# State-space layer of a two-layer trunk: weight split and C product taken off GpSimd, decay matrices from one masked addition per head

## The chip, the core and the metric

The kernel runs on one core of one Trainium2 chip. The core has a matrix engine (TensorE, PE in the profile; its weight loads, PEld, overlap its matmuls), a vector engine (VectorE, DVE), a scalar engine for activations (ScalarE, ACT), a general engine (GpSimd, POOL) and a queue that issues most transfers (SyncE, SP). Each engine works through its own instructions in order and waits on semaphores for the others. The metric is the time of one execution on the device in microseconds (us).

## The reference, cut to what matters

The reference is a trunk of two layers over 256 latent tokens and 256 context tokens of width 1024. Layer 0 is attention and a gated feed-forward net; layer 1 is a bidirectional state-space mixer (32 heads, 4 groups, state 128, chunks of 128 tokens) and a feed-forward net. The change is in the mixer. For each direction and chunk it computes

```python
cum = jnp.cumsum(dtc * a, axis=1)
seg = cum[:, :, None] - cum[:, None, :]
decay = jnp.exp(jnp.where(lower, seg, -jnp.inf))
cb = jnp.einsum('bign,bjgn->bijg', cc, bc)
w = cb[..., None] * decay * dtc[:, None]
y = jnp.einsum('bijgr,bjgrp->bigrp', w, xc)
y = y + jnp.einsum('bign,bgrpn->bigrp', cc, s) * jnp.exp(cum)[..., None]
to_end = jnp.exp(cum[:, -1:] - cum) * dtc
s = s * jnp.exp(cum[:, -1])[..., None, None] + jnp.einsum('bjgr,bjgn,bjgrp->bgrpn', to_end, bc, xc)
```

`dt` is a softplus of a projection, `x`, `B` and `C` come from a centred convolution and a silu. The context is scanned first and leaves the state `s`; the latent tokens go on from it. After that `y + d*x` is multiplied by `silu(z)`, normed, and projected.

## The kernel before, in words

Every weight matrix arrives as a stream of units of 128x1024 numbers (`load_raw`, line 244, on SyncE's queue, five buffers). Matmuls keep fp32 accuracy with a split in two parts: ScalarE copies a unit rounded (L232), and a second engine subtracts (L234), so that each step of a GEMM is three matmuls (L289 to L291). `pool_split` lists the units whose subtraction is on GpSimd instead of VectorE: all of the attention input, every second unit of the state-space input (`si`), the first two of the last feed-forward input (`f1i`). Two split buffers `ws` exist in the state-space layer.

The `si` GEMM has 41 column blocks: one for `dt`, four for B, four for C, then sixteen pairs of an x block (512 tokens) and a z block (256). A unit is one block. When a block is done, its function runs: `ssm_dt`, `ssm_B`, `ssm_C`, `ssm_x`, `ssm_z`. TensorE's side work (transposes, states, outputs) is put in a timed queue with `later` and comes between the steps of the GEMM.

`ssm_dt` makes `dt` with a polynomial, the cumulative sums `cum` with scans (L1117), stores them in memory (L1119), and makes the columns `ust` that are used as scalars per row. `ssm_x` for pair j asks for the spread cumulative sums of the next two heads (`cum_load`, L1183, tile `cumb`, four buffers), makes the convolved `xs` (L1019 twice with the tile `cacc`, then L1082), and calls `head_mats` for its two heads. Later it transposes `xs` on TensorE (`xps`, L1231), copies it (`xl`, `xw`, L1237), makes the state (`sps`, L1247), and adds up the output `y` from sixteen matmuls (L1264): eight with `wm` (the decay matrices times `CB`), eight with `ctl` (C times a decay). `finish_pair` then makes `u` from `y`, `xs` and `z`, its square for the norm (added on GpSimd, L1280) and the split `vv` for the output product `so`.

`head_mats` for one head makes four sums `xx` of cumulative sum, row column and mask (L1195, VectorE, 128x128 each), one exponential over them (L1198, ScalarE), two exponentials into `wm` (L1200, L1201), three into `ctl` (L1204 to L1206), the product of `ctl` with C on GpSimd (L1207), and on VectorE the sum of the two masked parts (L1208) and the product with `CB` (L1210). `wm` and `ctl` have four buffers, two pairs; a pair's matrices can be written when `y` of two pairs before has been read.

The order of the instructions on each engine is set by the tile framework from the program's order and priorities (the weight stream has a higher one), not by a table.

## Time and profile before

| | us |
|---|---|
| median of 3 runs (1229.09 to 1230.51) | 1229.57 |
| span of the profiled execution | 1228.7 |
| state-space input product, all blocks (first to last `si` matmul) | 681.8 to 968.1 |
| first and last `xs` (pairs 0 and 15) | 750.8 and 971.4 |
| output product `so` | 970.2 to 1021.6 |

The profile is one execution. A busy time is the union of an engine's instructions. The chain of work that ended last is followed back from the last instruction: each of its rows gives a start, a length, the engine and the line. A group's row gives the busy time and the mean of one instruction in ns, and behind the bar the time that its engine stood idle before it and who ended that. A tile's or line's row gives the shortest, median and longest duration in ns. A stretch's row gives its bounds, its length, and each engine's busy time in it with the number of instructions.

### The profile page before, as it was taken

To read this page: it belongs to the slowest core of one execution; us is meant where nothing else is said; L and a number is where in the kernel's file an instruction comes from. 1 tells how busy PE (TensorE), PEld (TensorE's weight loads), DVE (VectorE), ACT (ScalarE), POOL (GpSimd) and SP (SyncE) were. 2 spreads that over 40 slices of the span, in tenths; PEclk is the share of its full clock that TensorE was granted. 3 is DMA by queue.
4 is the path that set the end of the run, shared out by engine and by line. 5 is a ranking of instruction groups with operands and counts; after the bars stand their busy time and mean duration, and the time that the engine had idled before them with its cause. 6 is when DMAs were issued, how large, how long until landed. Compare 5 with 4: busy or idle time off the path is not lost.

```text
span 1228.7 us, 17902 instructions
## 1 busy us (share of the span) xinstructions
PE 1167.3 (95%) x6899; PEld 950.4 (77%) x6903; DVE 858.9 (70%) x1411; ACT 596.3 (49%) x1072; POOL 177.3 (14%) x122
## 2 busy tenths in 40 slices
PE   8999999999999999999999988888888899999997
PEld 5765556678888888888888976666666698999997
DVE  4568856545776877655663699888888766777654
ACT  4366655543633333332222756566656546555542
POOL 3331221100000000000000232333334202000000
PEclk9999999999999999999999998999999999999999
DMA  8622142422344555536663335433333255776651
GB/s 313 240 97 93 58 148 70 137 69 86 119 152 158 168 158 163 163 112 214 216 209 123 91 105 134 106 104 103 103 103 103 84 175 173 228 235 212 183 182 58
DMA packets 56677, 176.64 MB, mean 144 GB/s; under 512 B 5840, under 2 KB 15632, under 8 KB 56592
## 3 DMA queue, kind: packets, MB, share of 16 engines
q1 hardware_dynamic: 56016, 174.98, 45.1%
q8 instruction: 54, 0.88, 0.3%
q10 hardware_dynamic: 576, 0.52, 0.1%
q14 instruction: 31, 0.25, 0.1%
HBM read 174.37 MB, written 1.11 MB: 143 GB/s over the span
## 4 chain that ended last, share of the span: by engine, by line
PE 73%; DVE 20%; ACT 2%; DMA 2%; issue 1%; POOL 0%; DVEq 0%; ACTq 0%; POOLq 0%
PE f0i L289 6%; PE f0i L291 6%; PE f0i L290 6%; DVE xx L1195 4%; PE f1i L289 3%; PE f1i L290 3%; PE f1i L291 3%; PE ai L289 3%; PE ai L291 2%; PE y L1264 2%; PE f0o L291 2%; PE f0o L289 2%; PE ai L290 2%; PE f0o L290 2%; DVE ws L234 2%; DVE cacc L1019 2%
## 5 line engine op out<-in xcount | busy, mean ns | idle before, releaser
L232 ACT ACTIVATE ws<-raw 128x1024 fp32r<-128x1024 f32 x215 | 227.1, 1056 | 260.9 <-PE f0i L291 87.6
L234 DVE TENSOR_TENSOR ws<-raw,ws 128x1024 fp32r<-128x1024 f32 x175 | 214.4, 1225 | 101.4 <-ACT ws L232 100.5
L234 POOL TENSOR_TENSOR ws<-raw,ws 128x1024 fp32r<-128x1024 f32 x40 | 99.2, 2482 | 322.9 <-ACT ws L232 307.2
L289 PE MATMUL f0i<-h,ws 128*128 128x512 f32 x336 | 131.4, 391 | 0.0
L290 PE MATMUL f0i<-h,ws 128*128 128x512 f32 x336 | 130.9, 389 | 0.0
L291 PE MATMUL f0i<-h,ws 128*128 128x512 f32 x336 | 130.8, 389 | 0.0
L289 PE MATMUL si<-h,ws 128*128 128x256 f32 (+1 forms) x312 | 111.8, 358 | 5.6 <-DVE cacc L1019 5.1
L409 DVE SCALAR_TENSOR_TENSOR macc<-raw,cpad,macc 128x1024 f32<-128x1024 f32 x70 | 89.1, 1281 | 31.0 <-DMA raw<-mod_w 30.8
L291 PE MATMUL si<-h,ws 128*128 128x256 f32 (+1 forms) x312 | 106.5, 341 | 3.3 <-DVE ws L234 2.0
L290 PE MATMUL si<-h,ws 128*128 128x256 f32 (+1 forms) x312 | 106.3, 341 | 0.0
L289 PE MATMUL f1i<-h,ws 128*128 128x256 f32 x352 | 100.1, 286 | 0.0
L290 PE MATMUL f1i<-h,ws 128*128 128x256 f32 x352 | 99.6, 283 | 0.0
L291 PE MATMUL f1i<-h,ws 128*128 128x256 f32 x352 | 99.5, 283 | 0.0
L566 POOL TENSOR_TENSOR h<-ht,h 128x256 fp32r<-128x256 f32 x12 | 9.8, 820 | 460.3 <-DVE ws L234 363.5
L289 PEld LDWEIGHTS si<-h,ws 128*128 128x128 f32 x312 | 60.0, 192 | 18.3 <-issue 12.0
L289 PEld LDWEIGHTS f0i<-h,ws 128*128 128x128 f32 x336 | 63.1, 188 | 14.1 <-ACT hid L573 0.8
L291 PEld LDWEIGHTS f0i<-h,ws 128*128 128x128 f32 x336 | 63.1, 188 | 13.2
L290 PEld LDWEIGHTS f0i<-h,ws 128*128 128x128 f32 x336 | 63.1, 188 | 13.0
L289 PEld LDWEIGHTS f1i<-h,ws 128*128 128x128 f32 x352 | 67.9, 193 | 0.8 <-ACT hid L573 0.4
L291 PEld LDWEIGHTS si<-h,ws 128*128 128x128 f32 x312 | 59.6, 191 | 11.1 <-DVE ws L234 2.4
L1195 DVE SCALAR_TENSOR_TENSOR xx<-cumb,ust,msk 128x128 f32<-128x128 f32 x128 | 67.9, 579 | 0.0
L290 PEld LDWEIGHTS f1i<-h,ws 128*128 128x128 f32 x352 | 67.8, 192 | 0.0
(303 smaller groups left out, 2824.4 us busy)
## 6 DMA issues: line engine op xcount, KB each, us to landing
raw<-mod_w SPq DMA_DIRECT2D x80, 512.0 KB, 3.7
raw<-w_f0i SPq DMA_DIRECT2D x44, 512.0 KB, 3.9
raw<-w_f1i SPq DMA_DIRECT2D x44, 512.0 KB, 3.9
raw<-w_si SPq DMA_DIRECT2D x41, 512.0 KB, 3.6
raw<-w_f0o SPq DMA_DIRECT2D x22, 512.0 KB, 4.7
raw<-w_f1o SPq DMA_DIRECT2D x22, 512.0 KB, 3.7
raw<-w_ai SPq DMA_DIRECT2D x18, 512.0 KB, 4.2
raw<-mod_s SPq DMA_DIRECT2D x16, 512.0 KB, 5.3
```

The source lines that it names most:

```text
L232: ops = [nc.scalar.activation(out=hi, in_=r, func=AF.Copy)]
L234: ops.append(eng.tensor_tensor(out=s[:, 1].rearrange("p a b -> p (a b)"), in0=r, in1=hi.bitcast(F32), op=ALU.subtract))
L289: nc.tensor.matmul(ps, lhsT=s[:, 0, b], rhs=xh[:, 0:n], start=first, stop=False)
L290: nc.tensor.matmul(ps, lhsT=s[:, 0, b], rhs=xl[:, 0:n], start=False, stop=False)
L291: nc.tensor.matmul(ps, lhsT=s[:, 1, b], rhs=xh[:, 0:n], start=False, stop=last)
L409: nc.vector.scalar_tensor_tensor(out=acc, in0=raw, scalar=sc, in1=acc, op0=ALU.mult, op1=ALU.add)
L566: nc.gpsimd.tensor_tensor(out=lo, in0=t, in1=hi.bitcast(F32), op=ALU.subtract)
L1019: nc.vector.scalar_tensor_tensor(out=a, in0=b, scalar=cw[:, w:w + 1], in1=a, op0=ALU.mult, op1=ALU.add)
L1195: nc.vector.scalar_tensor_tensor(out=xx[:, d, jt], in0=cb[:, d, 128 * jt:128 * jt + 128], scalar=s(jt, d), in1=self.msk[:, d], op0=ALU.add ...
L1264: nc.tensor.matmul(y[c, 0:T], lhsT=lhs, rhs=rhs, start=(n == 0), stop=(n == 3))
```

## The change: what it does

- `pool_split` keeps only the attention input: the odd units of `si` and two of `f1i` are subtracted on VectorE. The product of `ctl` with C is on VectorE too.
- `cum` is now counted from the middle of the 256 tokens for both directions; rows of `dt` are ordered so that a direction's latent and context rows lie together, and four scans over 64 partitions take the place of eight over 32. The value at the middle (`mid`) is stored, spread to all partitions, and used as the bias of the `ctl` exponentials. The column for the row term is one for both cases, so `ust` has two parts in place of three.
- `head_mats` makes one masked addition of 128x512 per head, in place in `cumb` (now eight parts, the loaded four in the middle). The row term is the bias of the exponentials, which write `wm` directly, or `x2` for the parts to be added. A head has six exponentials, as before: four of 128x256 and two of 128x128 (before: one of 128x512, one of 128x256 and four of 128x128).
- `finish_pair` folds the gain into ScalarE's copy and one VectorE operation.
- `yacc` shares a buffer with the norm's accumulator; the zero tile of the warm-up matmuls is 128 wide and read four times.

```diff
-        self.pool_split = {i for i, u in enumerate(self.units) if u[0] == "w" and (u[1] == "ai" or (u[1] == "si" and u[2] % 2) or
-                                                                     (u[1] == "f1i" and u[2] < 2))}
+        self.pool_split = {i for i, u in enumerate(self.units) if u[0] == "w" and u[1] == "ai"}
...
     def ssm_dt(self, j, ps):
...
-        nc.vector.memset(one, 1.0)
-        for q in range(4):
-            r = slice(32 * q, 32 * q + 32)
-            for c in range(2):
-                cc = slice(128 * c, 128 * c + 128)
-                v = (lambda ap: ap[r, cc][:, ::-1]) if q % 2 else (lambda ap: ap[r, cc])
-                nc.vector.tensor_tensor_scan(out=v(cum), data0=one[r, cc], data1=v(da), initial=0.0, op0=ALU.mult,
-                                             op1=ALU.add)
-        nc.sync.dma_start(out=self.cumd, in_=cum[0:64])
+        nc.vector.tensor_scalar(out=lg, in0=dt, scalar1=1e-37, scalar2=None, op0=ALU.max)
+        nc.scalar.activation(out=lg, in_=lg, func=AF.Ln)
+        mid = sp.tile([P, 1], F32, name="dt_mid")
+        for q in range(2):
+            r = slice(64 * q, 64 * q + 64)
+            for c in (q, 1 - q):
+                cc = slice(128 * c, 128 * c + 128)
+                v = (lambda ap: ap[r, cc][:, ::-1]) if q else (lambda ap: ap[r, cc])
+                nc.vector.tensor_tensor_scan(out=v(cum), data0=self.cst("ones")[r], data1=v(da), initial=0.0,
+                                             op0=ALU.mult, op1=ALU.add)
+                if c == q:
+                    nc.vector.tensor_copy(mid[r], cum[r, 127 + q:128 + q])
+                    nc.vector.tensor_scalar(out=cum[r, cc], in0=cum[r, cc], scalar1=mid[r], scalar2=None,
+                                            op0=ALU.subtract)
+            rows = slice(64 * q, 64 * q + 32)
+            nc.sync.dma_start(out=self.cumd[32 * q:32 * q + 32], in_=cum[rows])
+            nc.sync.dma_start(out=self.midd[32 * q:32 * q + 32], in_=mid[rows])
+        nc.sync.dma_start(out=self.mid, in_=self.midd.rearrange("h o -> o h")[0].partition_broadcast(P))
...
     def cum_load(self, h):
         nc, sp = self.nc, self.sp
-        t = sp.tile([P, 2, T], F32, tag="cumb", bufs=4, name="cumb")
+        t = sp.tile([P, 8, P], F32, tag="cumb", bufs=4, name="cumb")
         src = self.cumd.rearrange("(d h) i -> h d i", d=2)[h]
-        nc.sync.dma_start(out=t, in_=src.partition_broadcast(P))
+        nc.sync.dma_start(out=t[:, 2:6].rearrange("p (d c) i -> p d (c i)", d=2), in_=src.partition_broadcast(P))
         return t
...
     def head_mats(self, h, cb):
...
-        xx = sp.tile([P, 2, 2, P], F32, tag="xx", bufs=2, name="xx")
-        for d in range(2):
-            for jt in range(2):
-                nc.vector.scalar_tensor_tensor(out=xx[:, d, jt], in0=cb[:, d, 128 * jt:128 * jt + 128],
-                                               scalar=s(jt, d), in1=self.msk[:, d], op0=ALU.add, op1=ALU.add)
-        xf = xx.rearrange("p a b c -> p (a b c)")
-        nc.scalar.activation(out=xf, in_=xf, func=AF.Exp)
-        w = sp.tile([P, 4, P], F32, tag="wm", bufs=4, name="wm")
-        nc.scalar.activation(out=w[:, 1], in_=cb[:, 0, 128:256], func=AF.Exp, bias=s(2, 0))
-        nc.scalar.activation(out=w[:, 2], in_=cb[:, 1, 0:128], func=AF.Exp, bias=s(2, 1))
-        ct = sp.tile([P, 2, T], F32, tag="ctl", bufs=4, name="ctl")
-        c4, b4 = (t.rearrange("p d (c i) -> p (d c) i", c=2) for t in (ct, cb))
-        nc.scalar.activation(out=c4[:, 0::3], in_=b4[:, 0::3], func=AF.Exp)
-        nc.scalar.activation(out=c4[:, 1], in_=b4[:, 1], func=AF.Exp, bias=cb[:, 0, 127:128])
-        nc.scalar.activation(out=c4[:, 2], in_=b4[:, 2], func=AF.Exp, bias=cb[:, 1, 128:129])
-        nc.gpsimd.tensor_tensor(out=ct, in0=ct, in1=self.CT[g].unsqueeze(1).to_broadcast([P, 2, T]), op=ALU.mult)
-        nc.vector.tensor_tensor(out=w[:, 0::3], in0=xx[:, 0], in1=xx[:, 1], op=ALU.add)
+        c4 = cb.rearrange("p (a c) i -> p a c i", c=2)
+        nc.vector.tensor_tensor(out=c4[:, 0::3], in0=c4[:, 1:3],
+                                in1=self.msk.unsqueeze(2).to_broadcast([P, 2, 2, P]), op=ALU.add)
+        w = sp.tile([P, 4, P], F32, tag="wm", bufs=4, name="wm")
+        x2 = sp.tile([P, 2, P], F32, tag="x2", bufs=2, name="x2")
+        nc.scalar.activation(out=w[:, 0:2], in_=cb[:, 0:4:3], func=AF.Exp, bias=s(0, 0))
+        nc.scalar.activation(out=x2[:, 0], in_=cb[:, 6], func=AF.Exp, bias=s(0, 1))
+        nc.scalar.activation(out=x2[:, 1], in_=cb[:, 1], func=AF.Exp, bias=s(1, 0))
+        nc.scalar.activation(out=w[:, 2:4], in_=cb[:, 4:8:3], func=AF.Exp, bias=s(1, 1))
+        ct = sp.tile([P, 2, T], F32, tag="ctl", bufs=4, name="ctl")
+        for d in range(2):
+            nc.scalar.activation(out=ct[:, d], in_=c4[:, 1 + d].rearrange("p a b -> p (a b)"), func=AF.Exp,
+                                 bias=self.mid[:, 32 * d + h:32 * d + h + 1])
+        nc.vector.tensor_tensor(out=w[:, 0::3], in0=w[:, 0::3], in1=x2, op=ALU.add)
         wf = w.rearrange("p a b -> p (a b)")
         nc.vector.tensor_tensor(out=wf, in0=wf, in1=self.CB[g].rearrange("p a b -> p (a b)"), op=ALU.mult)
+        nc.vector.tensor_tensor(out=ct, in0=ct, in1=self.CT[g].unsqueeze(1).to_broadcast([P, 2, T]), op=ALU.mult)
         return w, ct
...
     def finish_pair(self, j, st, y):
...
-        nc.vector.tensor_scalar(out=u, in0=u, scalar1=gg, scalar2=None, op0=ALU.mult)
-        self.split(self.vv[j], u, T)
+        hi, lo = self.vv[j][:, 0], self.vv[j][:, 1]
+        nc.scalar.activation(out=hi, in_=u, func=AF.Copy, scale=gg)
+        nc.vector.scalar_tensor_tensor(out=lo, in0=u, scalar=gg, in1=hi.bitcast(F32), op0=ALU.mult, op1=ALU.subtract)
```

The order on the engines moves with it. VectorE in the middle of the pairs, from the first instruction that waits for `y` (before: L1208; `u` is made from `y`, `zs` is the gated z):

```order
L1208 TENSOR_TENSOR wm<-xx 128x2x128 [waits PE_49]
L1208 TENSOR_TENSOR wm<-xx 128x2x128 [waits DVE_49,PE_49]
L1195 SCALAR_TENSOR_TENSOR xx<-cumb,ust,msk 128x128 [waits DMAHW7_49,DVE_49]
L1210 TENSOR_TENSOR wm<-wm,CB_5402 128x512 [waits Activation_49]
L1272 SCALAR_TENSOR_TENSOR u<-xs,prm,y 128x256 [waits PE_49]
L1210 TENSOR_TENSOR wm<-wm,CB_5402 128x512 [waits DVE_49,Activation_49]
L1274 SCALAR_TENSOR_TENSOR u<-u,zs 128x256 [waits DVE_49]
L1195 SCALAR_TENSOR_TENSOR xx<-cumb,ust,msk 128x128 x3
L1019 SCALAR_TENSOR_TENSOR cacc<-si_6911,scwh,cacc 128x2x255 [waits Activation_49]
L1282 TENSOR_SCALAR u<-u,prm 128x256 [waits Activation_49]
L1019 SCALAR_TENSOR_TENSOR cacc<-si_6911,scwh,cacc 128x2x255 [waits DVE_49]
L574 TENSOR_TENSOR vv_5410<-u,vv_5410 128x256 [waits Activation_49]
```

Four more L1195, one weight split and `xs` follow. The same place in the change, up to the row before `xs`:

```order
L1198 TENSOR_TENSOR wm<-wm,x_6921 128x2x128 [waits PE_49,Activation_49]
L1263 SCALAR_TENSOR_TENSOR u<-xs,prm,y 128x256 [waits PE_49]
L1200 TENSOR_TENSOR wm<-wm,CB_5404 128x512 [waits DVE_49]
L1265 SCALAR_TENSOR_TENSOR u<-u,zs 128x256 [waits DVE_49]
L1201 TENSOR_TENSOR ctl<-ctl,CT_5396 128x512 [waits Activation_49]
L234 TENSOR_TENSOR ws_6945<-raw_6719,ws_6945 128x1024 [waits Activation_49]
L1275 SCALAR_TENSOR_TENSOR vv_5412<-u,prm,vv_5412 128x256 [waits DVE_49,Activation_49]
L1019 SCALAR_TENSOR_TENSOR cacc<-si_6855,scwh,cacc 128x2x255 [waits Activation_49]
L1198 TENSOR_TENSOR wm<-wm,x_6934 128x2x128 [waits Activation_49]
L1019 SCALAR_TENSOR_TENSOR cacc<-si_6855,scwh,cacc 128x2x255 [waits DVE_49]
L1200 TENSOR_TENSOR wm<-wm,CB_5404 128x512 [waits DVE_49]
L234 TENSOR_TENSOR ws_6984<-raw_6814,ws_6984 128x1024 [waits DMAHW7_49,Activation_49]
```

The eight `xx` and the multiplication L1282 are gone, a second weight split and a C product (L1201) have come in, and the second head's sum (L1198) stands eight rows behind the first. Behind `xs` VectorE has the second C product, `zs`, a masked addition (L1186), the two `xw`, and the other masked addition. TensorE's order around `xps` and `y` is the same as before.

ScalarE at the same place, from the copy `xl` of the transposes; before:

```order
L1198 ACTIVATE xx<-xx 128x512 [waits DVE_49]
L1233 ACTIVATE xl<-xps 128x256 [waits PE_49]
L1200 ACTIVATE wm<-cumb,ust 128x128 [waits DMAHW7_49,PE_49]
L1201 ACTIVATE wm<-cumb,ust 128x128
L1200 ACTIVATE wm<-cumb,ust 128x128 [waits DMAHW0_49,PE_49]
L1201 ACTIVATE wm<-cumb,ust 128x128
L1204 ACTIVATE ctl<-cumb 128x2x128 [waits PE_49,Pool_49]
```

and now:

```order
L1224 ACTIVATE xl<-xps 128x256 [waits PE_49]
L1190 ACTIVATE wm<-cumb,ust 128x256 [waits DMAHW6_49,PE_49]
L1193 ACTIVATE wm<-cumb,ust 128x256
L1190 ACTIVATE wm<-cumb,ust 128x256 [waits DMAHW0_49,PE_49]
L1196 ACTIVATE ctl<-cumb,mid 128x256 [waits PE_49]
L1196 ACTIVATE ctl<-cumb,mid 128x256
L232 ACTIVATE ws_6945<-raw_6719 128x1024 [waits DMAHW4_49,PE_49]
L1270 ACTIVATE sq<-u 128x256 [waits DVE_49,Pool_49]
L1274 ACTIVATE vv_5412<-u,prm 128x256
L1015 ACTIVATE cacc<-si_6855,scwh 128x512
L1193 ACTIVATE wm<-cumb,ust 128x256
```

Before, only the unmasked parts were written into `wm` behind `y`, and the masked ones stood ready in `xx`; now all of `wm` is written behind `y`, and the second head's last part (the second L1193) comes after the split, the square, the gain and the convolution.

More of the change, by code (lines that the diff above doesn't have):

```diff
@@ L469, in spin @@
         for _ in range(n):
[L470 removed]
+            self.pin(self.nc.tensor.matmul(ps.rearrange("p (a b) -> p a b", b=P), lhsT=self.zero[:, 0:P], rhs=self.zero.unsqueeze(1).to_broadcast([P, 4, P]), start=True, stop=True))
     def pin(self, ins):
@@ L620, in run @@
                 nc.sync.dma_start(out=self.prm_t[:, 128:], in_=self.a["prm"][:, 128:])
-            self.zero = cp.tile([P, 512], BF16, name="zero")
+            self.zero = cp.tile([P, P], BF16, name="zero")
             nc.gpsimd.memset(self.zero, 0.0)
@@ L1042, in ssm @@
             self.vv = [sp.tile([P, 2, T], F32R, name=f"vv{j}") for j in range(KS)]
-            self.ust = sp.tile([P, 3, P], F32, name="ust")
-            self.yacc = sp.tile([P, T], F32, name="yacc")
+            self.ust = sp.tile([P, 2, P], F32, name="ust")
+            self.yacc = self.smallp.tile([P, 512], F32, tag="nacc", name="yacc")[:, 0:T]
             g = Gemm()
@@ L1092, in t @@
             return sp.tile([P, T], F32, tag=tag, bufs=4, name="dt_" + name)
-        x, e, s, s2, p = t("x", "wm"), t("e", "wm"), t("s", "wm"), t("s2", "wm"), t("p", "cumb")
-        nc.scalar.activation(out=x[0:64], in_=ps[0:64, 0:T], func=AF.Identity, bias=self.prm("dtb")[0:64])
-        nc.scalar.activation(out=x[64:128], in_=ps[64:128, T:512], func=AF.Identity, bias=self.prm("dtb")[64:128])
+        x, e, s, s2, p = t("x", "wm"), t("e", "wm"), t("s", "wm"), t("s2", "wm"), sp.tile([P, T], F32, tag="xs", bufs=2, name="dt_p")
+        for q in range(4):
+            r, c = slice(32 * q, 32 * q + 32), slice(T * (q % 2), T * (q % 2) + T)
+            nc.scalar.activation(out=x[r], in_=ps[r, c], func=AF.Identity, bias=self.prm("dtb")[r])
         nc.scalar.activation(out=e, in_=x, func=AF.Abs)
@@ L1119, in ssm_dt @@
-        nc.sync.dma_start(out=self.cumd, in_=cum[0:64])
-        U = x
-        end = sp.tile([P, 2], F32, name="cumend")
-        for q in range(4):
-            r = slice(32 * q, 32 * q + 32)
-            first, second = (128, 0) if q % 2 else (127, 255)
-            nc.vector.tensor_copy(end[r, 0:1], cum[r, first:first + 1])
-            if q >= 2:
-                c1, c2 = (1, 0) if q % 2 else (0, 1)
-                nc.vector.tensor_copy(end[r, 1:2], cum[r, second:second + 1])
-                nc.vector.tensor_tensor(out=end[r, 0:1], in0=end[r, 0:1], in1=end[r, 1:2], op=ALU.add)
-                for c, e in ((c1, 0), (c2, 1)):
-                    cc = slice(128 * c, 128 * c + 128)
-                    nc.scalar.activation(out=U[r, cc], in_=cum[r, cc], func=AF.Exp, scale=-1.0, bias=end[r, e:e + 1])
@@ L1144, in tr @@
+        nc.sync.dma_start(out=self.mid, in_=self.midd.rearrange("h o -> o h")[0].partition_broadcast(P))
+        U = x
+        nc.vector.tensor_tensor(out=U, in0=lg, in1=cum, op=ALU.subtract)
+        for q, end in ((1, T - 1), (3, 0)):
+            r = slice(32 * q, 32 * q + 32)
+            nc.scalar.activation(out=U[r], in_=U[r], func=AF.Exp, bias=cum[r, end:end + 1])
         def tr():
```

33 lines of the change are left out of this document (12 added, 21 removed).

## The prediction, as it was put on record before the run

> **What bounds the kernel now.** The page's first lines make TensorE look like the bound: it is busy 95% of the span. Read by stage the picture is another. I read the busy times by stretch first, for the three parts of the state-space layer: from the first convolutions to the first head, the sixteen pairs of heads, and the output product.
>
> ```profile
> PE 1167.3 (95%) x6899; PEld 950.4 (77%) x6903; DVE 858.9 (70%) x1411; ACT 596.3 (49%) x1072; POOL 177.3 (14%) x122
> core 0: us, PE busy (x) PEld busy (x) DVE busy (x) ACT busy (x) POOL busy (x), PEclk, DMA share, GB/s
> 704.00:751.00 47.00, 39.14 (x219) 33.65 (x217) 42.98 (x86) 27.15 (x47) 10.61 (x4) 0.93 0.39 123
> 751.00:971.00 220.00, 186.25 (x1071) 143.31 (x1070) 193.80 (x344) 137.62 (x324) 87.89 (x59) 0.95 0.37 103
> 971.00:1022.00 51.00, 50.05 (x416) 48.13 (x414) 31.96 (x49) 23.39 (x33) 3.83 (x3) 1.00 0.49 155
> ```
>
> In the pairs TensorE stands still for 34 us and VectorE for 26; in the output product TensorE is full. So a gain can come from the first two rows alone. Next the chain that ended last, over one pair, from one `xs` (the convolved x block) to the next:
>
> ```profile
> 855.04 0.61 DVE xs L1082
> 855.79 0.63 PE xps L1231 x4
> 857.11 1.06 PE y L1264 x8
> 859.10 0.68 DVE wm L1210
> 860.17 0.60 DVE wm L1210
> 861.11 3.42 DVE xx L1195 x3
> 864.53 0.66 DVE cacc L1019
> 865.19 0.65 DVE u L1282
> 866.42 0.85 DVE vv L574
> 867.27 1.05 DVE xx L1195 x4
> 868.32 1.14 DVE ws L234
> 869.46 0.61 DVE xs L1082
> PE xps L1231 <- DVE xs L1082: 31.1, 14, 2.6
> ```
>
> It is a loop of 14.42 us. VectorE's `xs` releases the transposes on TensorE, and `y` follows. The end of the first half of `y` (857.11 + 1.06 = 858.17) gives back the `wm` buffers, VectorE works through its queue in order for 11.3 us, and only then comes the next `xs`. The last row is the same thing as a wait: 31.1 of TensorE's 34 idle us are `xps` waiting for `xs`. Three instructions of the loop are far too long, and GpSimd is why:
>
> ```profile
> 846.99 2.54 POOL L234 TENSOR_TENSOR ws<-raw,ws 128x1024 fp32r<-128x1024 f32 x1 [10.16 <-ACT ws L232]
> 848.28 1.41 DVE L1282 TENSOR_SCALAR u<-u,prm 128x256 f32<-128x256 f32 x1
> L1195 DVE SCALAR_TENSOR_TENSOR xx<-cumb,ust,msk x128: 335/343/2492, 744.3 to 956.7; 128x128 f32<-128x128 f32 x128
> L574 DVE TENSOR_TENSOR vv<-u,vv x14: 404/856/1552, 774.0 to 968.4; 128x256 fp32r<-128x256 f32 x14
> L1207 POOL TENSOR_TENSOR ctl<-ctl,CT 128x512 f32<-128x512 f32 x32 | 43.5, 1376 | 23.4 <-ACT ctl L1206 23.4
> ```
>
> GpSimd's weight split ends at 849.53, and the VectorE multiplication that began under it ends at 849.69. An `xx` of normally 0.34 us takes up to 2.49. Work that looks free on GpSimd is paid in VectorE's queue.
>
> **The change, part by part.** The loop is summed first. Rows for what is not yet in a fence:
>
> ```profile
> L1210 DVE TENSOR_TENSOR wm<-wm,CB x32: 679/683/693, 749.7 to 964.2; 128x512 f32<-128x512 f32 x32
> L234 DVE TENSOR_TENSOR ws<-raw,ws x17: 1209/1212/1642, 741.7 to 969.9; 128x1024 fp32r<-128x1024 f32 x17
> L563 ACT ACTIVATE h<-ht,modT x8: 491/493/497, 690.1 to 696.4; 128x256 fp32r<-128x256 f32 x8
> 1026.60 1.31 ACT L563 ACTIVATE h<-ht,modT 128x256 fp32r<-128x256 f32 x3 [0.30 <-DVE ht L561]
> 855.79:870.21 14.42, 11.93 (x73) 9.42 (x73) 13.00 (x24) 8.90 (x21) 5.86 (x4) 1.00 0.38 110
> 870.21:885.82 15.61, 13.56 (x72) 10.12 (x73) 12.80 (x24) 9.17 (x21) 5.83 (x4) 0.89 0.33 101
> L1082 DVE SCALAR_TENSOR_TENSOR xs<-cth,cacc x16: 676/679/1747, 750.8 to 971.4; 128x512 f32<-128x512 f32 x16
> ```
>
> Between `y` and `xs` VectorE loses the eight `xx` (3.42 + 1.05 + one of about 0.26 = 4.74), the gain multiplication L1282 (0.65), and what the lock adds to `vv` (0.85 − 0.40 = 0.45): 5.84. It gains the second weight split of the pair (1.21), and the C product of the first head (0.68, priced as the 128x512 product L1210). It also gains a wait. Before, the exponentials of the masked sums were made ahead into `xx`, so the sum L1208 could start the moment `y` ended; now they go straight into `wm`, which `y` holds, so ScalarE has two 128x256 exponentials with a bias column to do first (priced as L563: 0.49, and 0.41 for the next, as three in a row took 1.31) = 0.90. Queued behind that waiting sum are the rest of the pair's VectorE work and `xs`. So 11.3 − 5.84 + 2.79 = 8.25, and with 3.1 from `xs` to the end of the first half of `y`, the loop is 11.4 us.
>
> Two masked additions and the second head's C product (three times 0.68 = 2.04) are costed at nothing: they stand in the 3.1 + 0.9 us in which VectorE otherwise waits for `xps` and `y`, beside `zs` (0.41) and `xw` (0.76) and the end of `xs`. That cover is nearly full: 0.68 + 2.04 + 0.41 + 0.76 = 3.9 of 4.0 us. Without it they cost 1.4 to 2.0 a pair. ScalarE's count hardly moves: out go two `xx` exponentials, four of `wm` and six of `ctl`, in come twelve, eight of them 128x256 with a bias, about +0.3 on 8.9 us.
>
> When the loop is that short, TensorE is late next. Its busy time in the undisturbed pair, 11.93 us, is the floor. I take 12.1 us a pair, the floor and 0.2 for hand-overs. The second pair in the fence shows what else goes: after the wait at `xps` its granted clock is 0.89 and it takes 15.61 us, and with no such wait I expect the clock to stay at 1.00. From the first to the last `xs` fifteen periods take 971.4 − 750.8 = 220.6 us, 14.7 each. At 12.1 they take 181.5: **−39 us**. The bounds are 11.7 (the ends of matmuls are modelled, so a little of 11.93 may overlap) and 13.4 (cover gone, 2.0 less the slack), that is −45 and −20.
>
> The stretch before it, 704 to 751, is VectorE's too:
>
> ```profile
> 723.57 3.17 POOL L234 TENSOR_TENSOR ws<-raw,ws 128x1024 fp32r<-128x1024 f32 x1 [4.29 <-ACT ws L232]
> 724.07 0.41 DVE L1104 TENSOR_TENSOR dt_p<-dt_p,dt_s 128x256 f32<-128x256 f32 x1
> 724.41 0.47 DVE L1019 SCALAR_TENSOR_TENSOR cacc<-si,scwh,cacc 128x255 f32<-128x255 f32 x1
> 724.80 2.08 DVE L1105 TENSOR_SCALAR dt_p<-dt_p 128x256 f32<-128x256 f32 x1
> L1105 DVE TENSOR_SCALAR dt_p<-dt_p 128x256 f32<-128x256 f32 x7 | 5.3, 758 | 0.0
> L1098 DVE TENSOR_SCALAR dt_s<-dt_e x1: 2285/2285/2285, 707.5 to 707.5; 128x256 f32<-128x256 f32 x1
> L1102 DVE TENSOR_SCALAR dt_p<-dt_s x1: 285/285/285, 713.9 to 713.9; 128x256 f32<-128x256 f32 x1
> L1117 DVE TENSOR_TENSOR_SCAN dt_s<-dt_p,dt_s x8: 386/396/2430, 732.6 to 737.2; 32x128 f32<-32x128 f32 x8
> 739.91 0.77 PE L289 MATMUL si<-h,ws 128*128 128x512 f32 x1 [3.93 <-DVE cacc L1019]
> ```
>
> Locks: L1105 5.3 − 7 × 0.29 = 3.3, L1098 2.0, one scan 2.0, together 7.3. Eight scans become four of twice the partitions, each priced at 0.40 since a scan runs along the row: −1.6. Four weight splits come over: 4 × 1.21 = +4.8. Net −4.1 on an engine that holds TensorE there (the wait of 3.93 us behind the scans). I take **−4**, from −8 (all of TensorE's idle 7.9 us in that row) to +1 (the locks were under other waits and only the splits count). The new transfers (two halves of the cumulative sums, two of the midpoints, one spread of them) follow the last weight load of that stretch on the DMA queue; the first C product needs the midpoints and stands well behind the first masked sum, so I cost them at nothing, or 2 us (one more store that a load waits for) where they hold the next weight load; that is inside the +1 bound and the range. The first two splits of the last feed-forward layer, the accumulator's shared buffer and the smaller zero tile fall where TensorE is full or spins: nothing.
>
> Sum: −39 − 4 = −43. The profiled execution's span is 1228.7 and the median of the runs 1229.57, so the same difference holds for both: **1186 us**.
>
> **A lock that stays.** GpSimd keeps one addition a pair, the accumulator:
>
> ```profile
> L1280 POOL TENSOR_TENSOR yacc<-yacc,sq 128x256 f32<-128x256 f32 x15 | 12.4, 824 | 19.5 <-ACT sq L1279 19.5
> ```
>
> Above, the split at 723.57 took 3.17 us against 2.54 of the other one: as I read the rows, it waited until VectorE came to `cacc` at 724.41, whose input `si` lies in PSUM, and VectorE's next pure SBUF operation then waited for it. The Trainium skill, "SBUF — State Buffer", section "Who interferes with whom", states this as an exclusive lock: a VectorE instruction with two SBUF inputs contends with a GpSimd one that reads SBUF, and the second to issue blocks until the first is finished. The trace agrees (the 2.08 us row). In the new order two instructions with two SBUF inputs stand right behind `sq`'s source and then `cacc`, which reads PSUM for 0.74 us, about as long as the addition lasts; so I cost the lock at nothing, and at 0.82 a pair if it falls on SBUF operations: the first rival.
>
> **Rivals.** (1) *The remaining lock falls on the loop*: 11.4 + 0.8 + hand-overs = 12.9 a pair, −27 − 4 = 1198. For it: VectorE will be denser. Against it: the `cacc` next to it. (2) *The cover fails*: the masked additions wait for their loads (`cumb`, about 5 us to land, asked for when ScalarE has done the previous exponentials) or for room, 13.4 a pair: −20 − 3 = 1206. (3) *Slower*: the waits on ScalarE become serial. If VectorE stands still until ScalarE has done the five exponentials behind `y` (2.2), split, square, gain, convolution and the second head's exponential (1.06 + 0.40 + 0.45 + 0.76 + 0.49), it loses 5.4 in place of 0.9: 15.9 a pair, +18 − 4 = 1243. It decides from a wait of about 4.2 us. Against it: the second head's sum stands eight instructions behind the first. (4) *The moved work eats the gain*, or the order does not do what it says: the locks end but equal work takes their place on a path I mis-read: 14.6 a pair, 1227 to 1231.
>
> **How the numbers follow.** Forecast 0.60 (its own range 1178 to 1194), rival 1 0.17, rival 2 0.15, slower 0.05, no change 0.03. The range reaches over both rivals of the same sign: 1174 to 1207. A measurement of this kernel can tell about 0.2% from no change (2.5 us): faster 0.92, same 0.03, slower 0.05.
>
> **What would show it.** Right: no VectorE instruction over 1.8 us in the pairs; `xps`'s wait for `xs` down from 31 to under 8 us; pairs of about 12.1 us without the alternation of 14.4 and 15.6; a granted clock of 1.00 there; the wait of 3.93 us behind the scans below 2. Wrong: VectorE idle in front of the sum L1198 for much more than 0.9 us (rival 3), in front of the masked addition on a DMA (rival 2), or stretched SBUF operations beside the accumulator's addition (rival 1).

## The result, and the profile after

The changed kernel takes 1189.99 us (median, 1189.60 to 1193.49) against 1230.04 (1229.09 to 1232.22) in the same session: a ratio of 0.9675, 95% interval 0.9659 to 0.9691. The forecast was 1186.0, in a range of 1174 to 1207. The profiled executions have spans of 1188.5 and 1228.7, a difference of 40.2 us, close to the 40.0 of the medians, so the traces can be set against each other term by term.

First the page of the changed kernel: the busy times of the span, and the shares of the engines in the chain that ended last.

```profile
PE 1160.5 (98%) x6902; PEld 950.5 (80%) x6902; DVE 826.6 (70%) x1341; ACT 604.1 (51%) x1072; POOL 88.9 (7%) x67
PE 88%; DVE 7%; ACT 2%; DMA 2%; issue 1%; POOL 0%; DVEq 0%; SPq 0%; ACTq 0%; POOLq 0%
```

Then its busy times by stretch, cut as before: from the first convolutions to the first `xs`, from there to the last `xs`, and the start of the output product. Columns are the stretch, its length, then busy us and instructions of PE, PEld, DVE, ACT and POOL, the granted clock, and the DMA share and GB/s.

```profile
704.00:753.64 49.64, 41.82 (x222) 36.69 (x221) 35.45 (x72) 30.34 (x51) 0.00 (x0) 0.87 0.36 116
753.64:931.30 177.66, 176.12 (x1076) 140.30 (x1076) 167.77 (x288) 142.27 (x322) 20.23 (x13) 1.00 0.50 129
931.30:981.60 50.30, 50.21 (x410) 47.91 (x409) 32.37 (x48) 23.05 (x33) 2.13 (x2) 1.00 0.50 157
836.73:931.25 94.52, 94.52 (x587) 74.56 (x586) 88.25 (x151) 73.99 (x166) 12.20 (x8) 1.00 0.49 124
```

The whole gain lies in the second row. From the first `xs` to the last, fifteen periods take 177.7 us in place of 220.6: **−42.9**. The first `xs` comes at 753.6 in place of 750.8: **+2.8**. From the last `xs` to the end it is 257.2 us in place of 257.3. The sum is −40.2. The row of the pairs before, cut at the same places, shows what the 42.9 are made of:

```profile
750.84:971.42 220.58, 186.83 (x1076) 143.87 (x1075) 194.38 (x345) 137.78 (x324) 87.89 (x59) 0.95 0.36 103
```

TensorE's idle time falls from 33.8 us to 1.5, and its busy time from 186.8 to 176.1 for the same 1076 matmuls, at a granted clock of 1.00 in place of 0.95. So about 32 us are waits that ended, and about 11 are the same matmuls done faster.

The last row for the changed kernel covers its last eight periods, 11.82 us each: TensorE is busy for all of 94.52 us, VectorE for 93% of it, and the clock stays at 1.00. Before, the same eight pairs read:

```profile
854.97:971.42 116.45, 99.27 (x584) 76.44 (x585) 100.54 (x178) 70.89 (x166) 44.59 (x31) 0.96 0.32 100
```

That is 14.56 us a pair with TensorE idle for 17 of 116 us. So the bound has moved from VectorE's loop to TensorE's work. The groups of the changed kernel show the rest: `xs` no longer has a stretched instance, TensorE's wait for it has gone from 31.1 us to 1.1, and one instruction is still stretched, `vv`.

```profile
L1084 DVE SCALAR_TENSOR_TENSOR xs<-cth,cacc x16: 676/679/687, 753.6 to 931.3; 128x512 f32<-128x512 f32 x16
  PE xps L1222: 1.1, 2
L1275 DVE SCALAR_TENSOR_TENSOR vv<-u,prm,vv x16: 485/959/971, 772.1 to 940.0; 128x256 fp32r<-128x256 f32 x16
L1271 POOL TENSOR_TENSOR yacc<-yacc,sq x15: 733/1525/1690, 783.1 to 939.8; 128x256 f32<-128x256 f32 x15
```

The front is where the forecast missed. VectorE and TensorE of the changed kernel in order of time there (start, duration, and in brackets the idle time before and what ended it):

```profile
725.22 0.55 PE L289 MATMUL si<-h,ws 128*128 128x256 f32 x1 [3.71 <-DVE cacc L1019]
746.71 0.69 DVE L1186 TENSOR_TENSOR cumb<-cumb,msk 128x512 f32<-128x512 f32 x1 [5.81 <-DMA cumb<-cumd]
748.48 2.08 PE L1166 MATMUL cbps<-CT,BT 128*128 128x256 f32 x4 [3.31 <-ACT CB L1168]
751.92 0.69 DVE L1186 TENSOR_TENSOR cumb<-cumb,msk 128x512 f32<-128x512 f32 x1 [1.95 <-DMA cumb<-cumd]
```

Its transfers, as SP issues them in order of time:

```profile
735.66 0.34 SPq L1130 DMA_DIRECT2D midd<-dt_mid  x1
736.43 1.00 SPq L1129 DMA_DIRECT2D cumd<-dt_s  x2
737.48 0.42 SPq L1130 DMA_DIRECT2D midd<-dt_mid  x1
741.95 0.39 SPq L1176 DMA_DIRECT2D cumb<-cumd  x1
744.36 0.35 SPq L1131 DMA_DIRECT2D mid<-midd  x1
```

And by line, with the size and the median time from issue to landing, of 733 to 765 us:

```profile
cumd<-dt_s SPq DMA_DIRECT2D x2, 32.0 KB, 4.3
midd<-dt_mid SPq DMA_DIRECT2D x2, 0.1 KB, 5.1
```

Before, one store of the sums went out at 734.09 and the first load of `cumb` at 736.11:

```profile
734.09 0.49 SPq L1119 DMA_DIRECT2D cumd<-dt_s  x1
736.11 0.39 SPq L1183 DMA_DIRECT2D cumb<-cumd  x1
```

So two suspects stand in the front: the transfers (2.0 us between store and load became 5.5, with VectorE idle 5.81 us at the first masked addition), and the weight splits that VectorE took over (TensorE's wait of 3.71 for `cacc`).

### The profile page after: what moved, and what is told of

It reads as the page before. It is cut to its first block, busy times and chain, and to the rows that moved or that the text cites. A ratio compares the mean times of both kernels' runs of the same rounds, so it can differ in the third digit from the quotient of the medians.

```text
span 1188.5 us, 17744 instructions
## 1 busy us (share of the span) xinstructions
PE 1160.5 (98%) x6902; PEld 950.5 (80%) x6902; DVE 826.6 (70%) x1341; ACT 604.1 (51%) x1072; POOL 88.9 (7%) x67
## 4 chain that ended last, share of the span: by engine, by line
PE 88%; DVE 7%; ACT 2%; DMA 2%; issue 1%; POOL 0%; DVEq 0%; SPq 0%; ACTq 0%; POOLq 0%
PE f0i L289 6%; PE f0i L290 6%; PE f0i L291 6%; PE si L289 4%; PE f1i L290 4%; PE f1i L291 4%; PE f1i L289 4%; PE si L291 3%; PE si L290 3%; PE f0o L289 3%; PE f0o L290 3%; PE f0o L291 3%; PE ai L289 3%; PE ai L291 2%; PE ai L290 2%; PE y L1255 2%
## 5 line engine op out<-in xcount | busy, mean ns | idle before, releaser
L234 DVE TENSOR_TENSOR ws<-raw,ws 128x1024 fp32r<-128x1024 f32 x197 | 240.7, 1222 | 101.8 <-ACT ws L232 100.4
L291 PEld LDWEIGHTS f0i<-h,ws 128*128 128x128 f32 x336 | 63.1, 188 | 13.2
L289 PEld LDWEIGHTS si<-h,ws 128*128 128x128 f32 x312 | 60.6, 194 | 14.8 <-issue 9.3
L289 PEld LDWEIGHTS f1i<-h,ws 128*128 128x128 f32 x352 | 67.3, 192 | 1.2 <-ACT h L563 0.7
L290 PEld LDWEIGHTS f1i<-h,ws 128*128 128x128 f32 x352 | 67.6, 192 | 0.5 <-DVE h L568 0.5
L291 PEld LDWEIGHTS f1i<-h,ws 128*128 128x128 f32 x352 | 67.6, 192 | 0.0
L291 PEld LDWEIGHTS si<-h,ws 128*128 128x128 f32 x312 | 60.4, 193 | 7.4 <-DVE ws L234 1.1
L290 PEld LDWEIGHTS si<-h,ws 128*128 128x128 f32 x312 | 60.7, 195 | 5.5
L289 PE MATMUL ai<-h,ws 128*128 128x512 f32 x144 | 62.5, 436 | 0.1
```

Of the source, the lines that this page charges most:

```text
L234: ops.append(eng.tensor_tensor(out=s[:, 1].rearrange("p a b -> p (a b)"), in0=r, in1=hi.bitcast(F32), op=ALU.subtract))
L289: nc.tensor.matmul(ps, lhsT=s[:, 0, b], rhs=xh[:, 0:n], start=first, stop=False)
L290: nc.tensor.matmul(ps, lhsT=s[:, 0, b], rhs=xl[:, 0:n], start=False, stop=False)
L291: nc.tensor.matmul(ps, lhsT=s[:, 1, b], rhs=xh[:, 0:n], start=False, stop=last)
```

## The experiments

All ratios are to the kernel before, run in the same session. For the pairs there are two readings: all fifteen periods, and the last eight, which the front no longer disturbs in the changed kernel and those near it. Line numbers shift by one to three between the changed kernel and its variants.

### The two halves apart

**GpSimd's work alone** (the kernel before, with this edit):

```diff
-  pool_split = ... u[1] == "ai" or (u[1] == "si" and u[2] % 2) or (u[1] == "f1i" and u[2] < 2)
+  pool_split = ... u[1] == "ai"
-  nc.gpsimd.tensor_tensor(out=ct, in0=ct, in1=self.CT[g]..., op=ALU.mult)
+  nc.vector.tensor_tensor(out=ct, in0=ct, in1=self.CT[g]..., op=ALU.mult)
```

> The kernel before, with one half of the change: the weight splits of the state-space stage and the first two of the last feed-forward layer, and the C products, go from GpSimd to VectorE; the decay matrices and the arithmetic of the cumulative sums stay as before. Theory A (the time went to VectorE instructions that were held while GpSimd worked): the eight xx come back to 0.34 us each (2.0 us less in the loop), L1282 and vv lose 0.8, one split and one C product come in (1.9), and the engine's whole work is about 13.4 us a pair: 13.4 to 13.8 us a pair in place of 14.7, and a front that is 2 us shorter, 1208 to 1214 us. Theory B (the gain lies in the smaller arithmetic of the decay matrices, and GpSimd's work was cover that is now paid in full): two splits and two C products (3.8 us) come on top of a loop that keeps its eight xx: 15 us a pair or more, 1232 us or more.

Measured: 1194.63 us, ratio 0.9716 (0.9694 to 0.9737).

**The arithmetic alone** (the changed kernel, with the same two lines turned back):

> The changed kernel, with the other half undone: the weight splits (state-space stage and first two of the last feed-forward layer) and the C products are back on GpSimd; decay matrices and cumulative sums as changed. Theory A: GpSimd works 6.1 us a pair (2.5 split, 2 x 1.4 products, 0.8 accumulator) and each masked addition, sum, product and vv that begins under it is held: single VectorE instructions over 1.8 us are back, 12.5 to 13.5 us a pair, 1200 to 1212 us. Theory B: 11.3 - 5.84 + 0.9 + 3.1 = 9.5 us of loop, so TensorE's 11.85 us a pair, as in the changed kernel: 1186 to 1191 us.

Measured: 1223.79 us, ratio 0.9951 (0.9936 to 0.9967). The busy times of the last eight pairs, first of the kernel with GpSimd's work moved, then of the one with the arithmetic alone:

```profile
832.93:935.30 102.37, 101.32 (x624) 80.16 (x623) 98.96 (x210) 73.11 (x169) 6.72 (x8) 1.00 0.44 125
```

```profile
861.07:969.60 108.53, 96.89 (x585) 73.78 (x585) 91.18 (x128) 74.44 (x166) 46.43 (x31) 1.00 0.38 108
```

Theory B falls: 87% of the gain (34.8 of 40.0 us) is there without touching the decay matrices. Theory A was right in kind and too small by 13 us (and 12.45 us a pair over all fifteen periods, where it gave 13.4 to 13.8): I had priced VectorE's work at 13.4 us a pair, and it is 12.4 (98.96 us in eight). The busy times of its groups of instructions add up to 112.9 us there; the rest is overlap between groups, for which I had taken off too little. An operation listed with 0.68 us holds up the next for 0.60, since the next begins before the end of the last (`xs` at 848.54 and `ctl` at 849.14, in a fence near the end). TensorE looks full in that row because its 624 matmuls hold 50 of the output product, into which it runs ahead; its end is 3 us longer all the same (260.2 us behind the last `xs`).

A plain rival is that GpSimd's results came late, and not that VectorE was held. The waits of before speak against it: in all fifteen periods TensorE waited 1.0 us for a result of GpSimd, and 30.7 us for VectorE's `xs`.

In the last eight pairs the four kernels make a clean square: 14.56 us a pair before, 12.80 without GpSimd's work, 13.57 with the new arithmetic, 11.82 with both. Each half is worth the same with and without the other (1.76 and 1.75; 0.99 and 0.98). Over all fifteen periods there is no such square: 14.7, 12.45, 14.9 and 11.84. And the arithmetic alone is worth only 5.7 us in all; theory A gave 1200 to 1212 us for it, and missed by 12. Its chain of waits begins the pairs like this:

```profile
742.95 8.80 DMA midd<-dt_mid
752.32 7.28 DMA cumb<-cumd
759.62 0.70 DVE cumb L1187
```

The midpoints' store, then the first load of `cumb`, then the first masked addition: VectorE stood idle there for 12.81 us. In this kernel the first `xs` (746.1) stands ahead of that wait, so the wait lies in the first of the fifteen periods, which takes 23.9 us. The load that spreads the midpoints stands ahead of the first load of `cumb` in SP's queue here (751.80 and 752.32) and waits 5.8 us for their stores; in the changed kernel it stands behind it (744.36 and 741.95). The new arithmetic came with transfers that ate its gain. The last run of this section tests that by itself.

**The arithmetic without its transfers** (the midpoints spread by TensorE, as in the section after next, and GpSimd's work back as before):

> The version with the midpoints spread by TensorE (1181.5 us), with the splits and the C products back on GpSimd: the new arithmetic alone, without its transfers of the midpoints. With those transfers and with GpSimd's work it took 1223.8 us, since the first load of cumb was issued at 752.3 us, 9.4 behind the stores; its last eight pairs took 13.57 us each in place of 14.56. Theory R (the new arithmetic saves about 1 us in every pair, and the midpoints' transfers hid it): 13.5 us a pair over all fifteen and no wait of more than 4 us at the first masked additions, 1205 to 1213 us. Theory N (the arithmetic is worth nothing while GpSimd works; the last eight pairs were shorter for the delay ahead of them): 14.3 us a pair or more, 1218 to 1226 us.

Measured: 1212.62 us, ratio 0.9866 (0.9846 to 0.9886), 11.2 us less than with the transfers. The first masked addition waits for its load 2.78 us in place of 12.81:

```profile
747.01 1.31 DVE L1184 TENSOR_TENSOR cumb<-cumb,msk 128x512 f32<-128x512 f32 x1 [2.78 <-DMA cumb<-cumd]
```

The fifteen periods, from `xs` at 743.1 to `xs` at 953.3, take 210.2 us, 14.0 each, half a microsecond more than theory R gave, because the first one is still 20.1; the time lies at the upper edge of R and outside N. So both halves are real, by the medians: GpSimd's work is worth 34.8 us with the old arithmetic and 31.2 with the new; the arithmetic, once its transfers are out of the way, is worth 17.9 us beside GpSimd's work and 13.2 without it (1194.63 against the 1181.46 us of the section after next).

### Which of GpSimd's operations

**Only the splits back on GpSimd** (the changed kernel with the old `pool_split`):

> The changed kernel, with only the weight splits back on GpSimd (odd units of the state-space stage, first two of the last feed-forward layer); the C products stay on VectorE. With both back the pairs took 14.9 us in place of 11.85. Theory L (what counts is how long one GpSimd instruction holds VectorE: 2.5 us for a split, 1.4 for a product): most of the 3 us come back with the splits, 13.5 to 14.5 us a pair, 1208 to 1222 us less about 6 that the front gains. Theory S (what counts is GpSimd's whole time, 2.5 against 2.8 us a pair): 12.5 us a pair, 1193 to 1198 us.

Measured: 1201.74 us, ratio 0.9764 (0.9747 to 0.9780).

**Only the C products back on GpSimd:**

> The changed kernel, with only the C products back on GpSimd; the weight splits stay on VectorE. Theory L: 12 to 12.5 us a pair, 1192 to 1200 us. Theory S: 2 x 1.4 us of GpSimd against 2 x 0.68 us that VectorE is spared, 12.6 us a pair or more, 1200 to 1205 us.

Measured: 1202.85 us, ratio 0.9774 (0.9756 to 0.9793). The last eight pairs, first with the splits back, then with the products back:

```profile
845.72:943.85 98.13, 95.04 (x584) 74.00 (x584) 88.30 (x144) 74.25 (x167) 24.65 (x15) 1.00 0.43 120
```

```profile
840.54:943.67 103.13, 94.71 (x585) 74.38 (x584) 90.75 (x135) 74.49 (x166) 30.16 (x24) 1.00 0.43 114
```

That is 12.27 and 12.89 us a pair. Over all fifteen periods it is 13.55 and 12.87. The readings part for the splits, since the first masked addition waits 12.59 us for a load there, behind the first `xs`, as in the run with the arithmetic alone: the first period takes 24.3 us. So by all fifteen the splits' run would lie in theory L's 13.5 to 14.5, and its total is 0.3 us below L's (1202 to 1216 with the 6 us of the front taken off). By the last eight, which that wait does not reach, theory L falls: the longer instruction costs less (0.45 us a pair against 1.07). Theory S is near there (it gave 12.5, and 12.6 or more) and has the total of the products' run, but it misses that of the splits' (1193 to 1198), and the cost is not in proportion to GpSimd's time. One pair of each shows the hold itself. With the splits back, VectorE and GpSimd in order of time:

```profile
851.51 0.68 DVE L1202 TENSOR_TENSOR ctl<-ctl,CT 128x512 f32<-128x512 f32 x1
852.69 2.03 DVE L1276 SCALAR_TENSOR_TENSOR vv<-u,prm,vv 128x256 fp32r<-128x256 f32 x1 [0.50 <-ACT vv L1275]
852.03 2.41 POOL L235 TENSOR_TENSOR ws<-raw,ws 128x1024 fp32r<-128x1024 f32 x1 [9.03 <-ACT ws L233]
```

`vv`, 0.48 us when nothing stands beside it (the run below without the accumulator on GpSimd), begins under the split and ends at 854.72, 0.28 us after the split's end at 854.44: it could not finish before GpSimd did. With the products back:

```profile
858.92 1.51 DVE L1265 SCALAR_TENSOR_TENSOR u<-u,zs 128x256 f32<-128x256 f32 x1
858.75 1.40 POOL L1201 TENSOR_TENSOR ctl<-ctl,CT 128x512 f32<-128x512 f32 x1 [6.99 <-ACT ctl L1196]
```

The same hold: `u` normally takes 0.42 us, and ends 0.28 us behind GpSimd's product here too. And there is a second cost that the splits do not have, in the waits of the eight pairs (who waited for whom, us in total, times, longest):

```profile
DVE cumb L1186 <- DMA cumb<-cumd: 8.7, 6, 2.1
```

That is 1.09 us a pair, as much as the whole loss; the splits' run has 0.7 us of it in all. I read this as the products' later end giving `ctl` and then `cumb` back later, so that the loads start later; no run tests that link.

The Trainium skill, "SBUF — State Buffer", section "Who interferes with whom", says that a VectorE instruction with two inputs in SBUF contends with a GpSimd instruction that reads SBUF, that the contention is an exclusive lock, and that the order of issue decides who blocks. The rows agree: `ctl` at 851.51, begun 0.52 us before the split, is not stretched, and `vv` and `u`, both with two inputs in SBUF and begun after GpSimd, end 0.28 us behind it.

### The front

**The midpoints without transfers.** The two stores and the spreading load go; one product against the identity spreads the column, beside the transposes of `ust`:

```diff
-  nc.sync.dma_start(out=self.midd[32 * q:32 * q + 32], in_=mid[rows])          (in the loop over q)
-  nc.sync.dma_start(out=self.mid, in_=self.midd.rearrange("h o -> o h")[0].partition_broadcast(P))
+  nc.tensor.matmul(p2[:, 256:384], lhsT=mid[:, 0:1].to_broadcast([P, P]), rhs=self.ident, ...)
-  bias=self.mid[:, 32 * d + h:32 * d + h + 1]
+  bias=self.ust[:, 2, 64 * d + h:64 * d + h + 1]
```

> The changed kernel, but the midpoints of the cumulative sums reach all partitions by one product on TensorE (the column repeated 128 times against the identity), next to the transposes of ust and evacuated with them; the two stores of the midpoints and the load that spreads them are gone, so that the first load of cumb stands directly behind the two stores of the sums. Theory C (the front lost its gain to the chain of small transfers in front of the first loads of cumb): the first cumb load is issued 2 to 4 us earlier, VectorE's idle 5.81 us at the first masked additions falls below 3, the first xs comes 3 to 5 us earlier than at 753.6, 1185 to 1187 us. Theory D (the front lost it to the four weight splits that now stand in VectorE's queue, with TensorE waiting 3.7 us for cacc): the first xs moves by less than 1 us, 1189 to 1191 us.

**The first splits back on GpSimd** (the odd ones of the first nine units of the stage; two of the four that VectorE had taken over in this stretch):

> The changed kernel, with the odd weight splits of the first nine units of the state-space stage back on GpSimd (the front stretch alone; the pairs keep theirs on VectorE). Theory D (the splits in VectorE's queue cost the front its gain): TensorE's wait of 3.7 us for cacc goes and the first xs comes 2 to 4 us earlier, 1186 to 1188 us. Theory C (the transfers did): locks come back into the long row of softplus operations, the transfers start as late or later, the first xs comes at 752 to 758, 1189 to 1195 us.

**Both together:**

> The changed kernel with both edits of the front: midpoints spread by TensorE, and the odd splits of the first nine units of the stage back on GpSimd. If the two losses of the front (the late loads of cumb, VectorE's four splits) lie one behind the other, the gains add: 1190 - 8.5 - 2.9 = 1178 to 1180 us. If they hide each other (whichever is late, the first masked addition waits for it), no more than the better of the two alone: 1181 to 1184 us.

Measured: 1181.46 us for the midpoints (ratio 0.9618, 0.9595 to 0.9640), 1187.11 for the splits (0.9652, 0.9632 to 0.9671), 1181.55 for both (0.9596, 0.9582 to 0.9611). SP and VectorE in order of time with the midpoints on TensorE:

```profile
735.06 1.01 SPq L1127 DMA_DIRECT2D cumd<-dt_s  x2
737.28 0.39 SPq L1173 DMA_DIRECT2D cumb<-cumd  x1
742.45 0.69 DVE L1183 TENSOR_TENSOR cumb<-cumb,msk 128x512 f32<-128x512 f32 x1 [2.60 <-DMA cumb<-cumd]
```

The landing of its stores, and the `xs` group:

```profile
cumd<-dt_s SPq DMA_DIRECT2D x2, 32.0 KB, 1.5
L1082 DVE SCALAR_TENSOR_TENSOR xs<-cth,cacc x16: 675/679/685, 747.6 to 923.5; 128x512 f32<-128x512 f32 x16
```

Theory C holds, and more than it asked: the stores land in 1.5 us in place of 4.3, the first load is issued 4.7 us earlier, VectorE's wait is down to 2.60, the first `xs` comes 6.0 us earlier, and the pairs lose their last 1.8 us of disturbance (175.9). By the medians it is 8.5 us less than the changed kernel, by the ratios 7.0, and the intervals lie apart. Theory D is right for a smaller part at most: with two splits back, TensorE's wait for `cacc` falls from 3.71 to 0.8 us and the stores go out at 733.0, but VectorE then waits 6.79 us for the same late transfers. The first `xs` comes at 746.8, earlier than either theory gave, but the period behind it takes 15.9 us, so that the last `xs` is only 3.1 us earlier. The time falls by 2.9 us between the medians, and the interval overlaps with that of the changed kernel. Both edits together have the median of the midpoints alone; by the ratios they are 2.7 us better, with intervals that overlap, so a further gain is not shown. In that run the stores go out at 734.77, only 0.3 us earlier than with the midpoints' edit alone; I have not followed why.

**The midpoints from another queue** (the changed kernel with both stores and the load issued by ScalarE):

```diff
-  nc.sync.dma_start(out=self.midd[...   /   nc.sync.dma_start(out=self.mid, ...
+  nc.scalar.dma_start(out=self.midd[... /   nc.scalar.dma_start(out=self.mid, ...
```

> The changed kernel, with the two stores of the midpoints and the load that spreads them issued from ScalarE's queue in place of SP's; the stores of the sums and the loads of cumb stay on SP's. Theory Q (the midpoints' stores hold up the stores of the sums because they stand among them in one queue): the stores of the sums land in about 1.5 us as without midpoints, the first cumb load is issued about 1.5 us behind them, 1181 to 1185 us. Theory M (the tiny stores and the strided load hold up the transfers wherever they are issued): the stores of the sums land in 4 us or more still, 1187 to 1191 us.

Measured: 1196.13 us, ratio 0.9717 (0.9698 to 0.9736): 6 us worse than the changed kernel, outside both theories. The wait for the stores in SP's queue:

```profile
SPq L1176 <- DMA cumd<-dt_s: 9.2, 1, 9.2
```

And the ScalarE instruction behind the load that spreads the midpoints:

```profile
741.41 0.66 ACT L1155 ACTIVATE Bk<-bps 128x256 f32<-128x256 f32 x2 [3.76 <-issue]
```

Theory Q falls: with the tiny stores out of SP's queue the sums' stores are waited for longer (9.2 us, where the changed kernel has 3.9), and they land after 7.0 us at the median. Theory M has that right and misses the time by 5 us. The first masked addition now waits 10.65 us for its load in place of 5.81, and ScalarE stands still 3.76 us before it may issue the load that needs the stores; this run does not part the two. The Trainium skill, "DMA: Bandwidth & Descriptors", section "Issuing engines are not separate DMA queues", says that transfers run on the same 16 engines and interleave whichever engine started them; this run agrees that another queue gave no way around.

### What bounds the pairs now

**The last addition off GpSimd** (the changed kernel with `yacc` added on VectorE):

> The changed kernel, with the last of GpSimd's work in the pairs, the addition into yacc, on VectorE. Theory A with rival 1 of the prediction (the remaining lock falls on the loop): vv, now 0.96 us in the pairs, returns to about 0.42, which pays for the addition's own 0.42, and a bound on VectorE would ease: 11.6 us a pair, 1184 to 1187 us. Theory T (TensorE's 11.82 us a pair is the bound now, and the lock lies beside it): vv returns to 0.42, but the pairs stay at 11.8 us and the time within 1.5 us of the changed kernel's 1190.

Measured: 1187.59 us, ratio 0.9644 (0.9623 to 0.9665).

Its `vv`, and its last eight pairs:

```profile
L1275 DVE SCALAR_TENSOR_TENSOR vv<-u,prm,vv x16: 471/478/484, 771.2 to 936.6; 128x256 fp32r<-128x256 f32 x16
```

```profile
833.64:927.49 93.85, 93.85 (x586) 75.34 (x586) 87.78 (x161) 74.42 (x170) 0.00 (x0) 1.00 0.49 127
```

`vv` returns from 0.96 to 0.48 us, which pays for the addition, and the last eight pairs go from 11.82 to 11.73 us (all fifteen from 11.84 to 11.66). The time lies between the two theories' ranges. The intervals overlap with those of the changed kernel, so the 2.4 us between the medians are not settled by these runs. The hold was there; its end moved the undisturbed period by 0.09 us.

**VectorE relieved by 1.36 us a pair** (the changed kernel without the C products; the state term of the output lacks its factor C):

> The changed kernel without the C products: ctl goes into y as the bare exponential, so the output lacks the factor C in the state term; it is a measure of time alone. VectorE is spared 2 x 0.68 = 1.36 us a pair, 20 us over the stretch. Theory T (TensorE's own work is the bound of the pairs now): the pairs stay at 11.6 to 11.8 us, and the time falls by no more than 3 us, to 1187 to 1190. Theory V (VectorE at 94% of the stretch still sets the period through its row between y and xs): 10.5 to 11.2 us a pair, 1170 to 1180 us.

Measured: 1186.17 us, ratio 0.9643 (0.9621 to 0.9665).

```profile
833.51:927.48 93.97, 93.91 (x587) 75.25 (x587) 79.64 (x135) 74.31 (x167) 11.18 (x8) 1.00 0.48 125
```

VectorE's busy time in the last eight pairs falls from 88.25 to 79.64 us and the period from 11.82 to 11.75: theory T, with a total just below its 1187. Theory V falls.

**Midpoints and accumulator together:**

> The version with the midpoints spread by TensorE (1181.5 us), with the addition into yacc on VectorE as well: no GpSimd work is left in the stage. If the last lock still costs the 2.4 us that its removal gave alone: 1178 to 1180 us. If that gain came from the same wait (the first pairs' late cumb loads) that the midpoints' edit has removed already: 1181 to 1182 us.

Measured: 1179.30 us, ratio 0.9579 (0.9561 to 0.9598), the fastest of all, 10.7 us under the changed kernel. Its interval just touches that of the midpoints alone, so the midpoints' edit is shown and the accumulator's share of 2 us is likely and no more.

## Why the prediction was right, and where it was not

**The bound before: right.** VectorE's loop set the pairs, and GpSimd's work was paid in VectorE's queue: moving that work alone gave 34.8 us. One reading under it is not what the row shows. The 2.08 us row was set beside a rule for instructions with two SBUF inputs, but `dt_p<-dt_p` has one. It ends at 726.88, 0.14 us behind GpSimd's split, so it was held; L1098 (2.29 us) and the gain multiplication L1282 (up to 2.48) were long with one SBUF tensor too. So in these traces the hold is not confined to two inputs.

**The pairs, −39 forecast, −42.9 measured: the mechanism right, the size a little low.** The fifteen periods are 11.84 each and the undisturbed ones 11.82, below the floor of 11.93 that I had read from one pair of before, and the 0.2 for hand-overs did not come: TensorE's chain runs from one pair into the next without a gap. The run without C products shows that TensorE is the bound and not VectorE at 93%. The loop of 11.4 that I worked out for VectorE was never on trial, since TensorE hid it.

**The cover: right.** The masked additions and the second C product do fit between `xs` and `y`. VectorE in order of time, in one pair, with what the wait in front of the sum was:

```profile
848.54 0.68 DVE L1084 SCALAR_TENSOR_TENSOR xs<-cth,cacc 128x512 f32<-128x512 f32 x1
849.14 0.68 DVE L1201 TENSOR_TENSOR ctl<-ctl,CT 128x512 f32<-128x512 f32 x1
851.34 0.68 DVE L1186 TENSOR_TENSOR cumb<-cumb,msk 128x512 f32<-128x512 f32 x1
852.67 0.42 DVE L1198 TENSOR_TENSOR wm<-wm,x 128x256 f32<-128x256 f32 x1 [0.66 <-ACT wm L1193]
```

The wait for ScalarE's exponentials is 0.66 us, forecast 0.9, and rival 3 (the waits in a row) did not come: the second head's sum has none.

**"The `cacc` next to it" (the lock that stays): wrong.** I costed the accumulator's addition at nothing because VectorE would be reading PSUM beside it, behind two instructions with two SBUF inputs. The order listed ahead of the prediction has three there: `ctl`, the split and `vv`. So `vv` is next to the addition, and not `cacc`:

```profile
854.95 1.22 DVE L234 TENSOR_TENSOR ws<-raw,ws 128x1024 fp32r<-128x1024 f32 x1
855.24 1.52 POOL L1271 TENSOR_TENSOR yacc<-yacc,sq 128x256 f32<-128x256 f32 x1 [10.29 <-ACT sq L1270]
856.08 0.96 DVE L1275 SCALAR_TENSOR_TENSOR vv<-u,prm,vv 128x256 fp32r<-128x256 f32 x1
```

The addition begins under VectorE's split, takes 1.52 us in place of the 0.73 of its shortest instance, and `vv` behind it takes 0.96 in place of 0.48. So rival 1 is half right: the lock falls on VectorE's queue, 0.5 us a pair where it had 0.8. It costs little because TensorE is later still, which the prediction did not say. Its 12.9 us a pair also holds 0.7 for hand-overs, without a source, where the forecast took 0.2.

**The front, −4 forecast, +2.8 measured: the step that failed.** The result lies outside the front's own bounds of −8 and +1. "I cost them at nothing, or 2 us": the transfers of the midpoints cost 7 to 8.5 us, shown by taking them away. I had placed the risk at the first C product, which needs the midpoints, and at the next weight load; it lay with the stores of the sums among which they stand, and so with the first load of `cumb` and the first masked addition. That is rival 2 ("the masked additions wait for their loads") in the front, where I had looked for it only in the pairs. The second failed term is "+4.8" for the splits, set against 7.3 us of ended locks as if they were exchanged on one engine. They were: VectorE's busy time there fell from 42.98 us to 35.45. TensorE's idle time did not (7.86 before, 7.82 after): the room went into waiting for transfers. The wait of 3.93 behind the scans, which I expected below 2, is gone as such; TensorE now waits 3.71 for `cacc` ahead of the scans, behind the splits, and 3.31 behind them, at 748.48. In TensorE's account the front's extra length is busy time, 39.14 before and 41.82 after, at a granted clock of 0.87 in place of 0.93; with the midpoints on TensorE it is 38.74, at 0.96. In this front the engine that was relieved gained only what the latest arrival allowed, and that was a transfer.

**The tail: right** (257.3 and 257.2 us), and of the signs named: no VectorE instruction over 1.8 us in the pairs, `xps` 1.1 (under 8), the clock 1.00, no alternation (the first seven periods still range from 10.6 to 13.1 us). The sign of the wait behind the scans was the one that failed. The two errors, 4 us too little in the pairs and 7 too much in the front, partly cancel, so it is luck that the total is nearer than its terms.

## What to carry to other kernels

Before work goes to GpSimd to relieve VectorE, look at VectorE's longest instances of operations that read SBUF: if they end just behind GpSimd's instruction, the work is not off the path, and taking it back onto VectorE can be faster even if VectorE then has more to do. Count every small store that is issued beside a store that something waits for; a spread of a column over the partitions can ride on a TensorE product that is there anyway. And when the engine that bounded a stretch is relieved, cost that stretch by its latest arrival, not by the busy time that an engine is spared.
